# Five small moves in the two mixers of a two-layer decoder step

## The chip, the cores and the metric

The kernel runs on one core of a Trainium2 chip. The metric is the device time of one execution in microseconds; the times below are medians over runs.

## The reference

One inference step of two layers, for 512 prompt rows and 64 sample rows (8 sequences of 8) that share all weights. Everything is float32.

Layer 0 has a mixer of two halves behind one input projection. Four retention heads: queries and keys are rotated, and o = intra + cross, a chunkwise linear attention with decay in chunks of 128 rows and a carried state; then o is normalised by `rsqrt(mean(o*o))` over its 128 channels and gated by silu(g). Four gMLP groups: a layer norm of gelu(gv), then within chunks of 128 rows `u * (tril(W_s) v + b)`. Both halves go through one output projection. Layer 1 is grouped attention with a window of 128, 16 query heads, 2 key/value heads and sinks. Each layer adds a residual, then an RMS norm and a squared-ReLU MLP with 4096 hidden channels, and another residual. A final RMS norm follows.

```python
h = x + mixer(rmsnorm(x))          # layer 0: mixer_ab, layer 1: swa
h = h + square(relu(rmsnorm(h) @ w_up)) @ w_down
o = o * rsqrt(mean(o*o) + eps); o_ret = silu(g) * o
o_gm = gelu(u) * (tril(w_s) @ layernorm(gelu(gv)) + b_s)
```

## The kernel before

All 576 rows lie along the free dimension, channels on the 128 partitions, in 8 chunks of 128 channels. To keep float32 precision, every operand of a large product is split into a high and a low part (`whi`, `wlo` for weights, `xhi`, `xlo` and so on for data), and a product is three matmuls: high x high, high x low, low x high. ScalarE casts the high part (L272 for weights), VectorE subtracts it from the source for the low part (L283). A weight piece is 128x512, two pieces make one chunk of output; six pieces can be held.

`gemm(xs)` makes one chunk of 128 output channels: 8 input chunks x 3 parts x 2 column halves of 288 = 48 matmuls. It writes an accumulator of two PSUM banks; there are two accumulators (tag acc), and four single banks (tag m) for everything else. `gemm` can be given other output banks by its argument `outs`, and functions to call between its input chunks by `mid`.

`chunk(xs, evac)` is one gemm, the evacuation of its accumulator, and then `stages()`, which calls what was put off with `later(d, fn)` until this many chunks on. So the small work of a head or a group is traced behind the large products of later chunks.

The program text is not the order in which an engine works. Outside the MLPs and one short stretch, where VectorE and ScalarE keep the order of the text, a planner sets the order of each engine's instructions, DMA issues included, when the kernel is built: it goes by its own model of durations and takes what its operands, buffers and banks allow, the earlier in the text first. On the chip each engine then runs its list in that fixed order and waits wherever an operand is late.

First mixer (`mixer0`): the chunks come as values 0, keys 0, values 1, queries 0, keys 1, queries 1, then values, keys and queries of heads 2 and 3, then `gv_out` of the four groups, `gate_out` of the four heads, `u_out` of the four groups, then the output projection. For a head, `scores` is traced one chunk after its queries, `mix` one chunk after that, and `normalise` one chunk after `mix`. `mix` leaves the head's output oT and its square osq (L886); `normalise` calls `mean_rsqrt`, which first splits osq into `sqh` (L220, ScalarE) and `sql` (L221, VectorE), multiplies both by a matrix of ones (L398, L399, TensorE) and takes the inverse root. Scaling oT by it is GpSimd's work, as are the sums of the rotations (L745), the decayed queries (L815) and the masked values vm (L783, for the samples' states). Work tiles of 576 columns share one tag with 21 slots.

For a group, `layernorm` is traced one chunk after `gv_out`: transposes to two single banks (L751), statistics, the normalised group gvn (L928, VectorE, out of the two banks), and GpSimd's scale and shift (L934, L936). gvn has three buffers. `spatial`, three chunks later, multiplies each group by the masked matrix wst (L945) and ws8, and VectorE adds the bias into om (L949, L952). The masks are two GpSimd products in place (L980, L982), traced right after the loads of wst and ws8, behind queries 0.

Second mixer (`mixer1`): the keys' chunk, then the values' chunk, both into accumulators, then query chunks 0 to 7. Within the values' gemm, at its fifth input chunk, `keys` is called: it finishes the norm, scales the keys (L1034), adds the bias and splits them. `v_out` scales the values (`scaled`, L1024), adds the bias (L1049), and puts off their transposes (L1054), which are traced within query chunk 0. Each query chunk belongs to one head of either key/value group. `scores` of a query chunk is traced two chunks on, `transpose_p` three chunks on, each in four parts, one for each half of the rows and key/value group; ScalarE copies the transposed probabilities of the first half out of PSUM (L1156), VectorE those of the second (L1158). `softmax` works in between (L1090 to L1105: maxima on VectorE, exponentials on ScalarE, the scaling on GpSimd). `values` is traced four chunks on.

Of the kernel before, what the change touches and what calls it, by code (L numbers as in the profile page):

```python
# [14 lines left out]
ALU = mybir.AluOpType  # L15
# [3 lines left out]
P = 128  # L19
# [3 lines left out]
NS = 64  # L23
# [96 lines left out]
def hybrid_step(ctx: ExitStack, tc: tile.TileContext, a, o):  # L120
# [6 lines left out]
    def halves(ap):  # L127
        return ap.rearrange("p (a b) -> p a b", a=2)

    def half(hf):  # L130
        return slice(hf * TH, (hf + 1) * TH)
# [232 lines left out]
    def later(d, fn):  # L364
        due.setdefault(slot[0] + d, []).append(fn)
# [10 lines left out]
    def chunk(xs, evac):  # L376
        evac(gemm(xs))
        stages()
# [8 lines left out]
    def two_parts(sq, temp):  # L387
        hi, lo = temp("sqh", F32R), temp("sql", F32R)
        split_into(sq, hi, lo)
        return hi, lo  # L390

    def mean_rsqrt(ones_r, sq, out, temp, parts_=None):

        hi, lo = parts_ or two_parts(sq, temp)
        r0, x = temp("rs0"), temp("rsx")
        for hf in range(2):
            ms = m_tile("ms")
            nc.tensor.matmul(ms[:, 0:TH], lhsT=ones_r, rhs=hi[:, half(hf)], start=True, stop=False)  # L398
            nc.tensor.matmul(ms[:, 0:TH], lhsT=ones_r, rhs=lo[:, half(hf)], start=False, stop=True)  # L399
            nc.scalar.activation(out=r0[:, half(hf)], in_=ms[:, 0:TH], func=AF.Abs_reciprocal_sqrt, bias=eps_r)  # L400
            nc.vector.scalar_tensor_tensor(out=x[:, half(hf)], in0=ms[:, 0:TH], scalar=RMS_EPS, in1=r0[:, half(hf)],
                                           op0=ALU.add, op1=ALU.mult)
        newton(x, r0, out)
# [273 lines left out]
    def mixer0(norm, nxt):  # L677
        with tc.tile_pool(name="mx0", bufs=2) as mp:
# [3 lines left out]
            def con(name):  # L682
                off, wd = C0W[name]
                return cst[:, off:off + wd]
# [173 lines left out]
            def mix(hd, qd, sd, sds, st, cxs):  # L858
                s0 = s0s[hd]
                (vt, vs, vms), (kt, k2) = vts[hd], kts[hd]  # L860
                g8 = float(pow_g(hd, DL))
                oT = w("oT")
                op_ = m_tile("op")
                for n in range(NB):
                    s_ = slice(n * P, (n + 1) * P)
                    nc.tensor.matmul(op_[:, s_], lhsT=vt[:, n, :], rhs=sd[:, n, :], start=True, stop=(n == 0))
                    if n > 0:
                        nc.tensor.matmul(op_[:, s_], lhsT=st[:, n - 1, :], rhs=qd[:, s_], start=False, stop=True)
                os_ = m_tile("os")
                nc.tensor.matmul(os_[:, 0:NS], lhsT=vs, rhs=sds, start=True, stop=False)  # L870
                for grp in range(2):
                    nc.tensor.matmul(os_[:, 32 * grp:32 * (grp + 1)], lhsT=cxs[:, grp, :], rhs=con("sel"),
                                     start=False, stop=(grp == 1))
                nc.scalar.copy(out=oT[:, 0:NP], in_=op_)
                nc.scalar.copy(out=oT[:, NP:T], in_=os_[:, 0:NS])
                for hf in range(2):
                    bs = slice(hf * 4, (hf + 1) * 4)
                    kvs = m_tile("kvs")
                    for i in range(2):
                        nc.tensor.matmul(kvs, lhsT=k2, rhs=vms[i][:, bs, :], start=(i == 0), stop=(i == 1))  # L880
                    nc.vector.scalar_tensor_tensor(out=s0[:, bs, :].rearrange("p b v -> p (b v)"),
                                                   in0=s0[:, bs, :].rearrange("p b v -> p (b v)"),
                                                   scalar=g8, in1=kvs, op0=ALU.mult, op1=ALU.add)
                nc.sync.dma_start(out=o["ret_s"][:, hd].rearrange("b d v -> d b v"), in_=s0)
                osq = w("osq")
                nc.scalar.activation(out=osq, in_=oT, func=AF.Square)  # L886

                def normalise():
                    ro = w("ro")
                    mean_rsqrt(ones_v, osq, ro, w)  # L890
                    nc.gpsimd.tensor_tensor(out=oT, in0=oT, in1=ro, op=ALU.mult)
                    ons[hd] = oT

                later(1, normalise)
# [17 lines left out]
            def layernorm(g, gz):  # L912
                tp, tq = to_tokens(gz)
                blocks = [(P, tp[:, n * P:(n + 1) * P]) for n in range(NB)] + [(NS, tq[0:NS, 0:P])]
                mv = mp.tile([P, NB + 1, 2], F32, name="mv", tag="mv")
                nc.gpsimd.memset(mv, 1.0)
                for n, (rows_, src) in enumerate(blocks):
                    bst = mp.tile([P, 6], F32, name="bst", tag="bst", bufs=4)
                    nc.vector.bn_stats(out=bst[0:rows_], in_=src)
                    nc.vector.bn_aggr(out=mv[0:rows_, n, :], in_=bst[0:rows_])  # L920
                var = mv[:, :, 1]
                r0, x, rl = (mp.tile([P, NB + 1], F32, name=n_, tag=n_) for n_ in ("rl0", "rlx", "rl"))
                nc.scalar.activation(out=r0, in_=var, func=AF.Abs_reciprocal_sqrt, bias=eps_l)
                nc.vector.scalar_tensor_tensor(out=x, in0=var, scalar=LN_EPS, in1=r0, op0=ALU.add, op1=ALU.mult)
                newton(x, r0, rl)
                gvn = mp.tile([P, NB + 1, P], F32, name="gvn", tag="gvn", bufs=3)
                for n, (rows_, src) in enumerate(blocks):
                    nc.vector.tensor_scalar(out=gvn[0:rows_, n, :], in0=src, scalar1=mv[0:rows_, n, 0:1],  # L928
                                            scalar2=rl[0:rows_, n:n + 1], op0=ALU.subtract, op1=ALU.mult)
                gs = slice(g * P, (g + 1) * P)  # L930
                for rows_, ns_ in ((P, slice(0, NB)), (NS, slice(NB, NB + 1))):
                    k = ns_.stop - ns_.start
                    v_ = gvn[0:rows_, ns_, :]
                    nc.gpsimd.tensor_tensor(out=v_, in0=v_, in1=ln_g[0:rows_, None, gs].broadcast_to([rows_, k, P]),  # L934
                                            op=ALU.mult)
                    nc.gpsimd.tensor_tensor(out=v_, in0=v_, in1=ln_b[0:rows_, None, gs].broadcast_to([rows_, k, P]),  # L936
                                            op=ALU.add)
                nc.sync.dma_start(out=o["gm"][:, gs], in_=gvn[0:NS, NB, :])
                later(3, lambda: spatial(g, gvn))

            def spatial(g, gvn):
                gs = slice(g * P, (g + 1) * P)
# [13 lines left out]
            def u_out(g, view):  # L956
# [20 lines left out]
            nc.sync.dma_start(out=wst, in_=a["wst"])  # L977
            ws8 = mp.tile([NS, NH, NS], F32, name="ws8", bufs=1)
            nc.sync.dma_start(out=ws8, in_=a["ws8"])
            nc.gpsimd.tensor_tensor(out=wst, in0=wst, in1=con("tri")[:, None, :].broadcast_to([P, NH, P]),  # L980
                                    op=ALU.mult)
            nc.gpsimd.tensor_tensor(out=ws8, in0=ws8,  # L982
                                    in1=con("tris")[0:NS, None, :].broadcast_to([NS, NH, NS]), op=ALU.mult)
            chunk(xs, lambda v: k_out(1, v))
            chunk(xs, lambda v: q_out(1, v))
            for hd in (2, 3):
                chunk(xs, lambda v: v_out(hd, v))
                chunk(xs, lambda v: k_out(hd, v))
                chunk(xs, lambda v: q_out(hd, v))
            for g in range(4):  # L990
                chunk(xs, lambda v: gv_out(g, v))
            for hd in range(4):
# [9 lines left out]
    def mixer1(norm, nxt):  # L1002
        with tc.tile_pool(name="mx1", bufs=2) as mp:
# [17 lines left out]

            def scaled(view):
                z = w("z")
                nc.vector.tensor_tensor(out=halves(z), in0=view, in1=norm.rv, op=ALU.mult)  # L1024
                return z

            kview = gemm(xs)
# [39 lines left out]

                later(1, tokens)

            v_out(gemm(xs, mid={4: [keys]}))  # L1070
            stages()


# [72 lines left out]
            def transpose_p(c, kv, np_):  # L1146
                s = ss[c, kv][0]
                if np_ == 0:
                    pts[c, kv] = mp.tile([P, NB, 2, P], F32, name="pT", tag="pT", bufs=3)
                tp = m_tile("tpp")  # L1150
                for i in range(1 if np_ == 0 else 0, 4):
                    n, hf = 2 * np_ + i // 2, i % 2
                    nc.tensor.transpose(out=tp[:, i * P:(i + 1) * P], in_=s[:, n, hf * P:(hf + 1) * P], identity=ident)  # L1153
                dst = pts[c, kv][:, 2 * np_:2 * np_ + 2].rearrange("p n h i -> p (n h i)")
                if np_ == 0:
                    nc.scalar.copy(out=dst[:, P:512], in_=tp[:, P:512])  # L1156
                else:
                    nc.vector.tensor_copy(out=dst, in_=tp)  # L1158

# [247 lines left out]
```

## Time and profile before

| | |
|---|---|
| Median of three runs | 1215.81 us (1213.68 to 1215.82) |
| Profiled execution | 1217.04 us; its span, first to last instruction, 1215.2 us |
| TensorE busy | 1190.1 us, 98% of the span |
| VectorE, ScalarE, GpSimd busy | 869.1, 576.8, 156.1 us |
| Mean granted TensorE clock | 0.994 of full speed |
| DMA | 109.42 MB, 90 GB/s over the span |

The span runs from the first to the last instruction of the profiled execution. Idle time of an engine is put down to what released it. In the span, the first mixer lies at about 0 to 268 us, the first MLP at 268 to 642, the second mixer at 642 to 826, the second MLP at 826 to the end.

### The profile page before, as it was taken

The page shows a single profiled execution, that of the slowest core. Times are in us where ns is not written, and L with a number is a line of the kernel's source. Part 1 is how long each engine was busy: PE and PEld are TensorE (multiplying, and loading weights), DVE is VectorE, ACT ScalarE, POOL GpSimd, SP SyncE. Part 2 cuts the span into 40 slices and gives each one's busy share as a digit, 9 for nine tenths or more (in the row PEclk, how much of TensorE's full clock was granted, in tenths as well). Part 3 has the DMA queues.
Part 4 walks back from the last instruction along what each step waited for, and adds up shares of the span by engine and source line. Part 5 has one row for each costly group of instructions (what it writes and reads, how often), then busy time and mean ns, then how long its engine had stood idle before and what let it go on. Part 6 is the DMA issues. An engine that isn't in the chain of part 4 may idle for free.

```text
span 1215.2 us, 22586 instructions
## 1 busy us (share of the span) xinstructions
PE 1190.1 (98%) x9177; PEld 1172.4 (96%) x9177; DVE 869.1 (72%) x1608; ACT 576.8 (47%) x1084; POOL 156.1 (13%) x137
## 2 busy tenths in 40 slices
PE   8999999999999999999999999999999999999996
PEld 8998999999999999999999989999999999999996
DVE  8967685447865875785796768646794795695696
ACT  6333554344443544453465777535453553453452
POOL 3443250110000000000001654120000000000000
PEclk9999999999999999999999999999999999999998
DMA  7244222222232232232223212122223132232222
GB/s 271 104 140 120 78 71 74 85 70 87 88 105 71 84 118 72 73 108 85 86 86 111 70 38 70 36 87 70 83 92 105 52 122 86 72 105 87 76 81 79
DMA packets 38263, 109.42 MB, mean 90 GB/s; under 512 B 4160, under 2 KB 12544, under 8 KB 38144
## 3 DMA queue, kind: packets, MB, share of 16 engines
q1 hardware_dynamic: 37440, 107.36, 28.7%
q8 instruction: 72, 1.18, 0.4%
q10 hardware_dynamic: 720, 0.62, 0.2%
q14 instruction: 31, 0.25, 0.1%
HBM read 102.92 MB, written 6.03 MB: 90 GB/s over the span
## 4 chain that ended last, share of the span: by engine, by line
PE 80%; DVE 11%; DMA 3%; ACT 3%; issue 2%; SPq 0%; DVEq 0%; ACTq 0%
PE acc L328 53%; PE acc L340 8%; PE f L340 3%; PE y L340 3%; PE w L340 3%; PE z L340 3%; DVE wlo L283 3%; DMA raw<-in_w_dn 2%; PE op L1166 1%; PE tpp L1153 1%; DVE alo L499 1%; PE sp L1134 1%; ACT ahi L498 1%; DVE h L547 1%; PE dn L328 1%
## 5 line engine op out<-in xcount | busy, mean ns | idle before, releaser
L328 PE MATMUL acc<-xhi,whi 128*128 128x288 f32 x1520 | 326.0, 296 | 2.6 <-DVE z L1034 2.2
L328 PE MATMUL acc<-xhi,wlo 128*128 128x288 f32 x1520 | 323.6, 294 | 0.0
L328 PE MATMUL acc<-xlo,whi 128*128 128x288 f32 x1520 | 322.5, 294 | 0.0
L283 DVE TENSOR_TENSOR wlo<-raw,whi 128x512 fp32r<-128x512 f32 x321 | 227.7, 722 | 80.9 <-ACT whi L272 79.4
L272 ACT CAST whi<-raw 128x512 fp32r<-128x512 f32 x321 | 191.4, 617 | 143.5 <-PE acc L328 109.5
L328 PEld LDWEIGHTS acc<-xhi,whi 128*128 128x128 f32 x1520 | 242.8, 189 | 4.3 <-issue 3.8
L328 PEld LDWEIGHTS acc<-xhi,wlo 128*128 128x128 f32 x1520 | 243.7, 188 | 0.3
L328 PEld LDWEIGHTS acc<-xlo,whi 128*128 128x128 f32 x1520 | 243.2, 188 | 0.0
L495 ACT ACTIVATE q<-t 128x576 f32<-128x576 f32 x64 | 43.9, 685 | 229.6 <-DVE t L490 229.6
L490 DVE SCALAR_TENSOR_TENSOR t<-acc,rstd 128x576 f32<-128x576 f32 x64 | 48.3, 755 | 82.9 <-PE acc L328 82.7
L272 ACT CAST whi<-s 128x512 fp32r<-128x512 f32 x124 | 73.7, 619 | 65.3 <-DVE s L257 55.8
L283 DVE TENSOR_TENSOR wlo<-s,whi 128x512 fp32r<-128x512 f32 x124 | 83.4, 683 | 10.6 <-ACT whi L272 10.6
L499 DVE TENSOR_TENSOR alo<-q,ahi 128x864 fp32r<-128x864 f32 x64 | 77.1, 1205 | 8.3 <-ACT ahi L498 8.3
L498 ACT CAST ahi<-q 128x864 fp32r<-128x864 f32 x64 | 66.5, 1038 | 13.6 <-DVE q L506 12.6
L340 PE MATMUL acc<-ahi,wlo 128*128 128x288 f32 x340 | 71.3, 298 | 0.6
L340 PE MATMUL acc<-ahi,whi 128*128 128x288 f32 x340 | 71.4, 295 | 0.0
L340 PE MATMUL acc<-alo,whi 128*128 128x288 f32 x340 | 70.3, 295 | 0.0
L257 DVE TENSOR_TENSOR s<-raw 128x512 f32<-128x512 f32 x62 | 42.5, 686 | 19.7 <-DMA raw<-in_w_dn 19.7
L1041 POOL TENSOR_TENSOR kl<-z,kh 64x512 fp32r<-64x512 f32 x4 | 5.5, 1365 | 394.4 <-ACT kh L1038 394.2
L340 PEld LDWEIGHTS acc<-ahi,wlo 128*128 128x128 f32 x340 | 53.6, 188 | 2.5 <-DVE wlo L283 2.5
L340 PEld LDWEIGHTS acc<-ahi,whi 128*128 128x128 f32 x340 | 54.0, 188 | 0.0
L340 PEld LDWEIGHTS acc<-alo,whi 128*128 128x128 f32 x340 | 53.7, 188 | 0.0
(329 smaller groups left out, 2090.5 us busy)
## 6 DMA issues: line engine op xcount, KB each, us to landing
raw<-in_w_up SPq DMA_DIRECT2D x64, 512.0 KB
raw<-in_w_dn SPq DMA_DIRECT2D x64, 512.0 KB
raw<-in_w_in SPq DMA_DIRECT2D x22, 512.0 KB
raw<-in_w_o SPq DMA_DIRECT2D x16, 512.0 KB
raw<-in_w_qkv SPq DMA_DIRECT2D x10, 512.0 KB
h<-in_xT SPq DMA_DIRECT2D x8, 288.0 KB
s<-in_s SPq DMA_DIRECT2D x4, 512.0 KB
out_ret_s<-s SPq DMA_DIRECT2D x4, 512.0 KB
```

The source lines that it names most:

```text
L257: nc.vector.tensor_tensor(out=sums[k, i], in0=x, in1=b[y], op=ALU.add)
L272: nc.scalar.copy(out=hi, in_=src)
L283: nc.vector.tensor_tensor(out=lo, in0=src, in1=hi.bitcast(F32), op=ALU.subtract)
L328: nc.tensor.matmul(out, lhsT=w_, rhs=x_[:, hf if isinstance(hf, slice) else half(hf)], start=(start and si == 0), stop=(stop and si == 2))
L340: nc.tensor.matmul(out, lhsT=w[wi][:, k * P:(k + 1) * P], rhs=x(k)[xi], start=(start and n == 0), stop=(stop and n == len(steps) - 1), ski ...
L490: nc.vector.scalar_tensor_tensor(out=halves(t), in0=view, scalar=0.0, in1=norm.rv, op0=ALU.max, op1=ALU.mult)
L495: nc.scalar.activation(out=flat(q[:, seg]), in_=t, func=AF.Square)
L498: nc.scalar.copy(out=hi[:, s0 - 1:s1 - 1], in_=q[:, s0:s1])
L499: nc.vector.tensor_tensor(out=lo[:, s0 - 1:s1 - 1], in0=q[:, s0:s1], in1=hi.bitcast(F32)[:, s0 - 1:s1 - 1], op=ALU.subtract)
L547: nc.vector.tensor_tensor(out=row[:, cols_], in0=row[:, cols_], in1=src, op=op)
L1134: nc.tensor.matmul(sp[:, i * 256 + 256 - wd:(i + 1) * 256], lhsT=q[kv][:, n * P:(n + 1) * P], rhs=kst[kv][part][:, lo:lo + wd], start=(par ...
L1153: nc.tensor.transpose(out=tp[:, i * P:(i + 1) * P], in_=s[:, n, hf * P:(hf + 1) * P], identity=ident)
```

## The change

Five places, none of which changes what is computed.

1. In `mixer0`, `mix` splits osq into its two parts at once, and hands them to `normalise`, which ran the split itself, a chunk later in the text.
2. `spatial` is put off four chunks instead of three.
3. The two mask products stand after the queries of head 3 instead of after the loads.
4. In `mixer1` the values' gemm writes two single banks (`vview`) instead of an accumulator; `scaled` then takes two instructions, one for each half.
5. In `transpose_p` the copy of the first half of the rows goes to VectorE for query chunk 0, once for each key/value group, and stays on ScalarE for the others.

```diff
@@ mix
                 nc.scalar.activation(out=osq, in_=oT, func=AF.Square)
+                osq_parts = two_parts(osq, w)
 
                 def normalise():
                     ro = w("ro")
-                    mean_rsqrt(ones_v, osq, ro, w)
+                    mean_rsqrt(ones_v, osq, ro, w, osq_parts)
@@ layernorm
-                later(3, lambda: spatial(g, gvn))
+                later(4, lambda: spatial(g, gvn))
@@ mixer0
-            nc.gpsimd.tensor_tensor(out=wst, in0=wst, in1=con("tri")[:, None, :].broadcast_to([P, NH, P]),
-                                    op=ALU.mult)
-            nc.gpsimd.tensor_tensor(out=ws8, in0=ws8,
-                                    in1=con("tris")[0:NS, None, :].broadcast_to([NS, NH, NS]), op=ALU.mult)
             chunk(xs, lambda v: k_out(1, v))
             chunk(xs, lambda v: q_out(1, v))
             for hd in (2, 3):
                 chunk(xs, lambda v: v_out(hd, v))
                 chunk(xs, lambda v: k_out(hd, v))
                 chunk(xs, lambda v: q_out(hd, v))
+            nc.gpsimd.tensor_tensor(out=wst, in0=wst, in1=con("tri")[:, None, :].broadcast_to([P, NH, P]),
+                                    op=ALU.mult)
+            nc.gpsimd.tensor_tensor(out=ws8, in0=ws8,
+                                    in1=con("tris")[0:NS, None, :].broadcast_to([NS, NH, NS]), op=ALU.mult)
@@ scaled
-                nc.vector.tensor_tensor(out=halves(z), in0=view, in1=norm.rv, op=ALU.mult)
+                if isinstance(view, list):
+                    for hf in range(2):
+                        nc.vector.tensor_tensor(out=z[:, half(hf)], in0=view[hf], in1=norm.rv[:, hf], op=ALU.mult)
+                else:
+                    nc.vector.tensor_tensor(out=halves(z), in0=view, in1=norm.rv, op=ALU.mult)
@@ mixer1
-            v_out(gemm(xs, mid={4: [keys]}))
+
+            vview = [m_tile("v1")[:, 0:TH] for _ in range(2)]
+            gemm(xs, vview, mid={4: [keys]})
+            v_out(vview)
@@ transpose_p
-                if np_ == 0:
+                if np_ == 0 and c:
                     nc.scalar.copy(out=dst[:, P:512], in_=tp[:, P:512])
+                elif np_ == 0:
+                    nc.vector.tensor_copy(out=dst[:, P:512], in_=tp[:, P:512])
                 else:
                     nc.vector.tensor_copy(out=dst, in_=tp)
```

## Rows read from the trace of the kernel before

**Rows 1.** The page's busy times, in us, with shares and counts.

```profile
PE 1190.1 (98%) x9177; PEld 1172.4 (96%) x9177; DVE 869.1 (72%) x1608; ACT 576.8 (47%) x1084; POOL 156.1 (13%) x137
```

**Rows 2.** TensorE's timeline: start, us, operation, count, [idle before it <- releaser].

```profile
47.08 1.13 PE L831 MATMUL kv<-vt,kt 128*128 128x128 f32 x8 [1.30 <-DVE v2l L779]
...
92.22 0.53 PE L399 MATMUL ms<-sql,ones_v 128*128 128x288 f32 x2 [1.14 <-DVE sql L221]
...
120.67 0.54 PE L399 MATMUL ms<-sql,ones_v 128*128 128x288 f32 x2 [1.13 <-DVE sql L221]
...
161.77 0.63 PE L751 MATMUL tp<-ident,gvz 128*128 128x128 f32 x4 [0.23 <-DVE gvn L928]
...
166.80 1.13 PE L945 MATMUL mx<-wst,gvn 128*128 128x128 f32 x8 [0.58 <-DVE om L952]
...
657.50 0.50 PE L328 MATMUL acc<-xhi,whi 128*128 128x288 f32 x2 [2.23 <-DVE z L1034]
...
703.57 1.12 PE L1153 MATMUL tpp<-ident,s 128*128 128x128 f32 x4 [2.43 <-ACT pT L1156]
```

**Rows 3.** Windows: stretch, its length, busy us by engine, granted clock, DMA.

```profile
658.00:664.00 6.00, 6.00 (x36) 6.00 (x36) 1.45 (x2) 3.93 (x7) 4.93 (x4) 0.72 0.33 90
703.00:708.00 5.00, 4.43 (x24) 4.44 (x25) 3.90 (x11) 2.52 (x7) 1.85 (x3) 0.66 0.00 0
46.00:48.00 2.00, 0.92 (x8) 0.95 (x8) 1.96 (x5) 0.00 (x0) 0.00 (x0) 1.00 0.00 0
268.00:650.00 382.00, 381.48 (x2894) 379.62 (x2893) 288.20 (x497) 180.62 (x305) 0.00 (x0) 1.00 0.29 88
```

**Rows 4.** Timeline at the head of the second mixer.

```profile
656.59 0.76 DVE L1034 TENSOR_TENSOR z<-acc,rstd 128x576 f32<-128x576 f32 x1
...
657.87 0.75 DVE L1024 TENSOR_TENSOR z<-acc,rstd 128x576 f32<-128x576 f32 x1
...
662.43 0.78 ACT L1049 ACTIVATE z<-z,cols 128x576 f32<-128x576 f32 x1
...
663.71 0.60 PE L1054 MATMUL tp<-ident,z 128*128 128x128 f32 x4
```

**Rows 5.** Timeline of ScalarE, VectorE and GpSimd ahead of the 2.43 us gap.

```profile
690.31 0.83 ACT L1156 COPY pT<-tpp 128x384 f32<-128x384 f32 x2
...
691.14 1.83 POOL L1105 TENSOR_TENSOR s<-s,den 128x128 f32<-128x128 f32 x2 [0.37 <-ACT pT L1156]
...
691.70 1.81 DVE L283 TENSOR_TENSOR wlo<-raw,whi 128x512 fp32r<-128x512 f32 x1 [0.71 <-ACT whi L272]
...
693.43 0.68 DVE L1158 COPY pT<-tpp 128x512 f32<-128x512 f32 x1
...
697.94 0.40 ACT L1093 ACTIVATE s<-s,nmax 128x128 f32<-128x128 f32 x1 [0.88 <-DVE nmax L1090]
```

**Rows 6.** Timeline from the square of head 1 to its low part.

```profile
78.99 0.69 ACT L886 ACTIVATE osq<-oT 128x576 f32<-128x576 f32 x1
...
80.09 1.90 POOL L783 TENSOR_TENSOR vm<-v2h,cst 128x1024 fp32r<-128x1024 f32 x1 [0.65 <-DVE wlo L283]
...
83.25 1.15 DVE L283 TENSOR_TENSOR wlo<-raw,whi 128x512 fp32r<-128x512 f32 x1 [2.06 <-ACT whi L272]
...
87.79 0.66 ACT L220 CAST sqh<-osq 128x576 fp32r<-128x576 f32 x1
...
90.33 1.83 DVE L221 TENSOR_TENSOR sql<-osq,sqh 128x576 fp32r<-128x576 f32 x1
```

**Rows 7.** Timeline of GpSimd and VectorE around the masks.

```profile
13.14 0.15 POOL L916 MEMSET mv<- 128x10 f32 x2
...
36.19 1.74 POOL L980 TENSOR_TENSOR wst<-wst,cst 128x512 f32<-128x512 f32 x1
...
39.53 5.58 DVE L803 TENSOR_TENSOR k<-ks__513,k 64x128 fp32r<-64x128 f32 x1
...
57.88 0.27 DVE L803 TENSOR_TENSOR k<-ks__726,k 64x128 fp32r<-64x128 f32 x1
```

## Prediction, made before the changed kernel was run

> **What bounds the kernel now.** I read four views, from coarse to fine. First the page's busy line [rows 1]: TensorE is busy 1190.1 of the span's 1215.2 us, so all that can be won without taking matmuls away is 25 us, less what the start and the end need. Second the TensorE timeline, of which only the rows with idle time ahead of them matter [rows 2]. The seven inside the two mixers are what the five edits can reach: 1.30, 1.14, 1.13, 0.23 and 0.58 us in the first mixer, 2.23 and 2.43 us in the second, 9.04 us in all. Each names who ended it, always VectorE or ScalarE letting go of a PSUM bank or delivering an operand; no weight load and no DMA is among them. Third, windows around these gaps [rows 3]. After the 2.23 us gap the granted clock averages 0.72 over 6 us, so 6 x 0.28 = 1.7 us more is lost; after the 2.43 us gap it averages 0.66 over 5 us, 1.7 us, of which up to 0.57 is idle time already counted, so I take 1.4. The stretch with the 1.30 us gap stays at 1.00. So the two long gaps cost 3.9 and 3.8 us, the five short ones only themselves: 12.1 us in all. For scale, the first MLP, with no gap of note, runs 2894 matmuls in 382 us, 0.132 us each, so a chunk of 48 takes 6.3 us. Fourth, the other engines around each gap [rows 4 to 7].
>
> The reader must keep in mind that a planner sets each engine's order from readiness in its own model. The first two memsets of the layer norms ran at 13.14 us [rows 7], ahead of the first head's work. So an edit of the text moves an instruction only if its operands or its slot held it back.
>
> **Part by part, in the size of the prize.**
>
> *Values in single banks.* The third product of the second mixer (query chunk 0) needs one of two accumulators, and both are held: the keys' until z at L1034 (656.59 + 0.76 us), the values' until z at L1024 [rows 4]. TensorE idles 2.23 us [rows 2]. With the values in two of the four single banks, query chunk 0 takes the accumulator that the MLP has let go, and starts at once. No matmul is added. VectorE does the values' scaling in two instructions instead of one of 0.75 us; even at twice that it adds 0.75 us, hidden while TensorE works through 6.3 us of query chunk 0, and the bank it holds longer is asked for only by the transposes that read its own result. Gain 2.23 + 1.7 = 3.9 us. Lower bound 0: the next thing late is the values' activation L1049 (ready at 662.43 + 0.78 = 663.2), on which the transposes L1054 wait [rows 4]; that is a rival below.
>
> *One copy on VectorE.* The 2.43 us gap ends when the copies at L1156 free a bank [rows 2]; they stand behind a row of exponentials on ScalarE that begins at 697.94 [rows 5]. These are copies of query chunk 1; the edit moves those of chunk 0, two instructions that take 0.83 us of ScalarE at 690.31. What they delay is seen in the same rows: the weight split on VectorE begins at 691.70 and takes 1.81 us beside a GpSimd product, then a copy, which ends at 694.1, then the scaling of query chunk 3, its maxima, and the exponentials. If ScalarE is free 0.83 us sooner, this chain comes 0.83 us sooner; if the split then also gets ahead of the GpSimd product, 1.81 goes to about the 0.68 that its neighbour takes [rows 5], another 1.1 us. VectorE pays two copies of 384 columns. The 512-column copy took 0.68, so an estimate from this row is 0.5 us each, 1.0 in all; the planner can set them before the chunk's end, and if that cover is gone they eat the 0.83. A gap of 0.5 to 1.6 us remains, near the 1.30 one that cost no clock. So the gain lies between 0.83 + 1.4 = 2.2 and 1.9 + 1.4 = 3.3; I take 2.2. Bounds 0 and 3.8.
>
> *Heads' squares split sooner.* In head 1 the square ends at 78.99 + 0.69 = 79.7 us, but its high part is made only at 87.79, and the low part begins at 90.33 and takes 1.83 us [rows 6]. The mean's second matmul waits 1.14 us for it; head 2 repeats this with 1.13 [rows 2]. ScalarE was not full in those 8 us, so something other than its operands held the high part, and its place in the program, one chunk on, is the likely one: slots of the shared work pool seem to be given out in program order. Traced right behind the square, both parts are ready several microseconds ahead of the matmul. Nothing is added; two work tiles live a chunk longer. Gain 2.27. Lower bound: the low part now falls beside GpSimd's masked values (80.09) [rows 6], the second rival.
>
> *Spatial products a chunk later.* They free TensorE from waiting for the sums before them (0.58), and the transposes from waiting for banks held by them (0.23) [rows 2]: gain 0.81. But only three buffers hold the normalised groups, so group 3's norm must now wait for group 0's product. TensorE comes to that product where group 1's stood, 166.80 to 167.9 [rows 2]. VectorE ended group 2's norm at about 161.7, which is what released the transposes at 161.77 [rows 2], and group 3's comes a chunk of at least 6.3 us later, 168 or after. So the wait is hidden behind the work that VectorE has before that norm, and costs nothing; if VectorE is early, it is at most a chunk of 6.3 us on VectorE.
>
> *Masks later.* On GpSimd the mask of wst took 1.74 us at 36.19, in a row of GpSimd work during which VectorE's 64-partition subtraction at L803 took 5.58 us; the same line otherwise took 0.27 [rows 7]. That subtraction pushes the one that ends the 1.30 us gap [rows 2]. Without the mask the row would be shorter and the gap smaller. But the masks need only their load, the planner put them where GpSimd had nothing else ready, and a later place in the program changes neither. So I take 0; bound 1.30.
>
> **Sum.** 3.9 + 2.2 + 2.3 + 0.8 + 0 = 9.2 us. The profiled execution took 1217.04 us (1.84 beyond its span); the median of the three runs is 1215.81. From the median: 1206.6 us. The same case with all its upper bounds wins the whole 12.1: 1203.7; with the copy's gain at 0 and the squares' at half, 5.9, it gives 1210.0. A change of 0.2% is 2.4 us, about what a measurement of this kernel can tell from none.
>
> **Rivals.**
>
> *The gap moves to the transposes.* In favour: the vector and scalar work behind the keys does not get faster, and the values' activation is ready at 663.2, while TensorE, 3.9 us sooner, would reach the transposes (now at 663.71) at 659.8 [rows 4], so it would wait up to 3.4 us, and the dip of the clock would follow as it does now. Against: the planner sees the same lateness in its model and can put the rest of query chunk 0 ahead of the transposes. The first edit then gives nothing: 1215.8 - 5.3 = 1210.5 us.
>
> *Slower: the low parts meet GpSimd.* VectorE's low part, issued beside the masked values at 80.09, would be held as L803 was, 5.58 less its own 0.27, or 5.3 us; VectorE's idle time there is 2.06 [rows 6], so 3.2 us would reach the rotations and weight splits behind it, in each of four heads: 12.8 us, against 6.9 won elsewhere: 1215.8 + 5.9 = 1221.7 us. It decides from 1.7 us a head. Against: TensorE has 6.3 us of matmuls a chunk and split weights in hand, so a late VectorE must be later than that. The low part of head 1 in the trace took 1.83 us and not 5.58 [rows 6].
>
> The Trainium skill (SBUF — State Buffer, Who interferes with whom) bears on this rival: a VectorE instruction with two SBUF inputs and a GpSimd instruction that reads SBUF exclude each other, and the one issued second waits until the first has finished. By that rule a low part would be held for one masked product of 1.90 us, less than the idle 2.06 us, and the rival would give the forecast's time. The trace disagrees in L803's row: 5.58 us, about three times the longest GpSimd instruction in these rows. The price above goes by the row.
>
> *No change.* The planner puts squares, copies and spatial products where they were, or orders the rest so that other waits open; 1214 to 1218 us. In favour: order is not the text's. Against: the accumulator is a resource, not an order, and it alone is worth more than 2.4 us.
>
> **Chances.** The forecast 0.60 (its own range 1203.7 to 1210.5), the moved gap 0.19 (1209 to 1213), no change 0.12, slower 0.09. Faster by over 0.2%: 0.79; within: 0.12; slower: 0.09. A range of 1203.5 to 1214.5 leaves out the slower case, half of no change and a little of the forecast.
>
> **What would show it.** No gap at the start of query chunk 0 and a granted clock of 1.00 around it; the high part of each square directly behind the square, and no wait at the mean's second matmul; no wait at the spatial products; the masks still at 36 us and the 1.30 us gap still there; the 2.43 us gap under 1.6 without a dip of the clock. It is wrong if a gap of over 2 us shows at the values' transposes, if low parts of over 3 us show beside GpSimd with TensorE idle behind, or if new gaps add up to more than 3 us.

## The result: 1208.3 us after 1215.1, and the profile after

| | before | after |
|---|---|---|
| Median, run side by side | 1215.07 us (1213.68 to 1215.82, 4 runs) | 1208.33 us (1207.19 to 1210.16, 4 runs) |
| Profiled execution, its span | 1217.04, 1215.2 us | 1207.19, 1205.4 us |
| Mean granted TensorE clock in it | 0.994 | 0.998 |

The ratio is 0.993, 95% interval 0.9915 to 0.9946: faster by 0.5% to 0.9%. The forecast was 1206.6 us in 1203.5 to 1214.5, so the range holds and the middle is 1.7 us too low. All runs of the study pooled, before has a median of 1216.31 us (40 runs, lowest 1213.68) and after one of 1208.33 (10 runs, lowest 1206.82). The medians of the table are 6.7 us apart, the pooled ones 8.0, and the interval of the ratio reaches from 6.6 to 10.3 us: the times alone give the gain to about 2 us.

The page's busy line answers to [rows 1]:

```profile
PE 1186.1 (98%) x9177; PEld 1169.3 (97%) x9177; DVE 872.6 (72%) x1611; ACT 576.4 (48%) x1082; POOL 157.6 (13%) x137
```

The same 9177 matmuls take 4.0 us less busy time: matmuls at half clock count as longer. Of TensorE's timeline, what is left of the seven gaps of [rows 2]:

```profile
47.05 1.13 PE L831 MATMUL kv<-vt,kt 128*128 128x128 f32 x8 [1.30 <-DVE v2l L779]
...
86.64 0.30 PE L399 MATMUL ms<-sql,ones_v 128*128 128x288 f32 x1
...
650.69 0.43 PE L328 MATMUL v<-xhi,wlo 128*128 128x288 f32 x2
650.96 0.42 PE L328 MATMUL acc<-xhi,whi 128*128 128x288 f32 x2
...
658.05 0.66 PE L1059 MATMUL tp<-ident,z 128*128 128x128 f32 x4 [1.07 <-ACT z L1054]
...
695.38 0.66 PE L1161 MATMUL tpp<-ident,s 128*128 128x128 f32 x4 [1.07 <-ACT pT L1164]
```

The mean's second matmul follows the first without a wait. Query chunk 0 (into acc, 650.96) follows the values (into v) directly. Gone are 1.14, 1.13, 0.23, 0.58 and 2.23 us; 2.43 has become 1.07; a new wait of 1.07 stands at the values' transposes; 1.30 is untouched. The seven gaps of 9.04 us are now three of 3.44. The window with the new wait, which answers to the first of [rows 3], shows no loss of clock:

```profile
655.00:661.00 6.00, 4.93 (x39) 4.69 (x39) 2.07 (x4) 4.71 (x10) 5.37 (x4) 1.00 0.31 98
```

So the profiled span is 9.8 us shorter: 5.6 in gaps, 3.1 in clock that is no longer lost, and 1.1 outside these waits. Most of this 1.1 is in the first mixer: TensorE comes to the mean of the first MLP's norm (L398) at 263.24 us instead of 267.21, 3.97 sooner, and the waits that are gone there are 1.14 + 1.13 + 0.23 + 0.58 = 3.08 of it. What the rest consists of I did not locate.

ScalarE's timeline around the new wait, and GpSimd's, VectorE's and ScalarE's around the squares and the copies, which answer to [rows 4 to 6]:

```profile
654.15 2.53 ACT L1043 CAST kh<-z 64x512 fp32r<-64x512 f32 x4
656.71 0.62 ACT L272 CAST whi<-raw 128x512 fp32r<-128x512 f32 x1
657.23 0.77 ACT L1054 ACTIVATE z<-z,cols 128x576 f32<-128x576 f32 x1
...
79.02 0.69 ACT L886 ACTIVATE osq<-oT 128x576 f32<-128x576 f32 x1
79.80 0.68 ACT L220 CAST sqh<-osq 128x576 fp32r<-128x576 f32 x1
...
80.19 1.90 POOL L783 TENSOR_TENSOR vm<-v2h,cst 128x1024 fp32r<-128x1024 f32 x1 [0.64 <-DVE wlo L283]
...
81.21 1.49 DVE L221 TENSOR_TENSOR sql<-osq,sqh 128x576 fp32r<-128x576 f32 x1
...
684.09 0.55 DVE L1166 COPY pT<-tpp 128x384 f32<-128x384 f32 x1
...
684.64 0.66 DVE L283 TENSOR_TENSOR wlo<-raw,whi 128x512 fp32r<-128x512 f32 x1
...
694.85 0.85 ACT L1164 COPY pT<-tpp 128x384 f32<-128x384 f32 x2
```

The values' bias is in ScalarE's queue behind four key casts and a weight cast. The high part of the square stands right behind the square, and the weight split after the moved copy takes 0.66 us, not 1.81. And GpSimd and VectorE, which answer to [rows 7]:

```profile
36.16 1.74 POOL L987 TENSOR_TENSOR wst<-wst,cst 128x512 f32<-128x512 f32 x1
...
39.49 5.58 DVE L803 TENSOR_TENSOR k<-ks__513,k 64x128 fp32r<-64x128 f32 x1
...
46.33 0.57 DVE L779 TENSOR_TENSOR v2l<-tq,v2h 64x128 fp32r<-64x128 f32 x2
```

The masks are where they were, and VectorE's subtraction at L803 takes 5.58 us as before.

### The profile page after: what moved, and what is told of

It is laid out like the page before. It is cut to its first block, busy times and chain, and to the rows that moved or that the text cites. A ratio compares the mean times of both kernels' runs of the same rounds, so it can differ in the third digit from the quotient of the medians.

```text
span 1205.4 us, 22593 instructions
## 1 busy us (share of the span) xinstructions
PE 1186.1 (98%) x9177; PEld 1169.3 (97%) x9177; DVE 872.6 (72%) x1611; ACT 576.4 (48%) x1082; POOL 157.6 (13%) x137
## 4 chain that ended last, share of the span: by engine, by line
PE 82%; DVE 10%; ACT 3%; DMA 3%; issue 2%; SPq 0%; DVEq 0%; ACTq 0%
PE acc L328 54%; PE acc L340 8%; PE f L340 3%; PE y L340 3%; PE w L340 3%; PE z L340 3%; DVE wlo L283 2%; DMA raw<-in_w_dn 2%; ACT s L1101 1%; PE tpp L1161 1%; DVE alo L499 1%; PE op L1176 1%; DVE h L547 1%; PE sp L1142 1%; ACT ahi L498 1%
## 5 line engine op out<-in xcount | busy, mean ns | idle before, releaser
L328 PE MATMUL acc<-xhi,whi 128*128 128x288 f32 x1504 | 321.4, 295 | 0.4 <-DVE vz L765 0.4
L328 PE MATMUL acc<-xhi,wlo 128*128 128x288 f32 x1504 | 319.0, 293 | 0.0
L328 PE MATMUL acc<-xlo,whi 128*128 128x288 f32 x1504 | 318.7, 293 | 0.0
L283 DVE TENSOR_TENSOR wlo<-raw,whi 128x512 fp32r<-128x512 f32 x321 | 232.2, 736 | 76.2 <-ACT whi L272 74.7
L328 PEld LDWEIGHTS acc<-xhi,whi 128*128 128x128 f32 x1504 | 239.3, 188 | 1.6 <-issue 1.2
L328 PEld LDWEIGHTS acc<-xhi,wlo 128*128 128x128 f32 x1504 | 240.4, 188 | 0.3
L328 PEld LDWEIGHTS acc<-xlo,whi 128*128 128x128 f32 x1504 | 240.0, 188 | 0.0
L499 DVE TENSOR_TENSOR alo<-q,ahi 128x864 fp32r<-128x864 f32 x64 | 77.1, 1205 | 8.3 <-ACT ahi L498 8.3
```

The lines of the kernel that those rows point to most:

```text
L283: nc.vector.tensor_tensor(out=lo, in0=src, in1=hi.bitcast(F32), op=ALU.subtract)
L328: nc.tensor.matmul(out, lhsT=w_, rhs=x_[:, hf if isinstance(hf, slice) else half(hf)], start=(start and si == 0), stop=(stop and si == 2))
L499: nc.vector.tensor_tensor(out=lo[:, s0 - 1:s1 - 1], in0=q[:, s0:s1], in1=hi.bitcast(F32)[:, s0 - 1:s1 - 1], op=ALU.subtract)
```

## The experiments

**One part undone at a time.** Four kernels, each the changed one with one of its parts taken back; run side by side, with before at a median of 1216.75 us.

Values back in an accumulator:

```diff
-            vview = [m_tile("v1")[:, 0:TH] for _ in range(2)]
-            gemm(xs, vview, mid={4: [keys]})
-            v_out(vview)
+            v_out(gemm(xs, mid={4: [keys]}))
```

> The changed kernel with the values' product back in an accumulator. Theory that each edit is worth its own gap: the 2.23 us gap at the start of query chunk 0 is back, with the dip of the clock behind it (1.7 us), and the 1.07 us gap at the values' transposes goes: 1208.3 + 2.2 - 1.1 + 1.7 = 1211.2 us. Rival, that the gap only moved from the accumulator to the transposes: at most 0.5 us either way, 1208.3 us.

Measured: 1210.46 us (1209.81 to 1211.8; ratio to before 0.9951, 0.9933 to 0.9968). TensorE's timeline, then two windows:

```profile
653.37 0.51 PE L328 MATMUL acc<-xhi,whi 128*128 128x288 f32 x2 [2.13 <-DVE z L1039]
```

```profile
653.00:659.00 6.00, 5.63 (x31) 5.66 (x32) 1.75 (x4) 4.16 (x7) 4.06 (x4) 0.72 0.32 90
760.00:768.00 8.00, 8.00 (x92) 6.93 (x89) 2.09 (x6) 1.64 (x7) 1.82 (x2) 0.79 0.01 2
```

The gap returns in place of the wait at the transposes, with a dip of 0.28 x 6 = 1.7 us behind it. The second row shows a dip of the same size (0.21 x 8) at 760 us, where before's profile and after's have none, and no gap of over 0.3 us ahead of it.

Squares split where they were, inside `mean_rsqrt`:

```diff
-                osq_parts = two_parts(osq, w)
-                    mean_rsqrt(ones_v, osq, ro, w, osq_parts)
+                    mean_rsqrt(ones_v, osq, ro, w)
```

> The changed kernel with the heads' squares split in normalise again. Theory of own gaps: 1.14 and 1.13 us come back at the mean's second matmul in heads 1 and 2, no dip: 1208.3 + 2.3 = 1210.6 us. Rival, that the early low parts cost VectorE beside GpSimd what they save TensorE: 1208.3 us or less.

Measured: 1210.25 us (1208.99 to 1213.15; ratio 0.9949, 0.9931 to 0.9968). TensorE's timeline, and a window:

```profile
92.23 0.53 PE L399 MATMUL ms<-sql,ones_v 128*128 128x288 f32 x2 [1.14 <-DVE sql L221]
...
120.69 0.54 PE L399 MATMUL ms<-sql,ones_v 128*128 128x288 f32 x2 [1.13 <-DVE sql L221]
```

```profile
762.00:768.00 6.00, 6.00 (x59) 5.28 (x61) 1.87 (x6) 1.61 (x6) 0.50 (x1) 0.72 0.00 0
```

Both waits are back to the hundredth, and a dip at 762 us stands in this profile too.

Spatial products three chunks on:

```diff
-                later(4, lambda: spatial(g, gvn))
+                later(3, lambda: spatial(g, gvn))
```

> The changed kernel with the spatial products three chunks on again. Theory of own gaps: 0.58 and 0.23 us come back in front of the second spatial product and of group 3's transposes: 1208.3 + 0.8 = 1209.1 us. Rival, that the wait of group 3's norm for a buffer costs more than that: 1208.3 us or less.

Measured: 1210.39 us (1210.12 to 1211.89; ratio 0.995, 0.9932 to 0.9969), more than expected. TensorE's timeline:

```profile
159.63 0.63 PE L751 MATMUL tp<-ident,gvz 128*128 128x128 f32 x4 [0.80 <-DVE gvn L929]
...
164.66 1.13 PE L946 MATMUL mx<-wst,gvn 128*128 128x128 f32 x8 [0.58 <-DVE om L953]
```

1.38 us of waits return, of which 0.80 is at the transposes where before had 0.23: without the squares' wait ahead of it, TensorE comes to the transposes sooner (the kernel before with only the squares' waits gone, below, has the same 0.80). A gap behind another one is larger once the first is gone.

The copies of query chunk 0 back on ScalarE:

```diff
-                if np_ == 0 and c:
+                if np_ == 0:
                     nc.scalar.copy(out=dst[:, P:512], in_=tp[:, P:512])
```

> The changed kernel with query chunk 0's copies on ScalarE again. Theory of own gaps: the gap at the transposes of query chunk 1 grows from 1.07 to 2.43 us and brings back its dip of 1.4 us: 1208.3 + 2.8 = 1211.1 us. Rival, that this gap shrank because the second mixer starts earlier by the values' edit: no change, 1208.3 us.

Measured: 1209.07 us (1207.84 to 1211.97; ratio 0.9941, 0.9922 to 0.996). TensorE's timeline and a window:

```profile
697.54 0.66 PE L1161 MATMUL tpp<-ident,s 128*128 128x128 f32 x4 [2.43 <-ACT pT L1164]
```

```profile
697.00:703.00 6.00, 5.46 (x44) 5.46 (x45) 5.93 (x17) 3.70 (x9) 3.17 (x4) 1.00 0.16 25
```

The gap is back at its old size, with the values' edit still in, so it was the copies and not the earlier start that had shrunk it. The clock stays at 1.00. The price of this edit is here the gap alone, 1.36 us, of which the medians show 0.7; with a spread of 4 us between runs that is no disagreement, and no proof either.

What the four give beside 1208.33 us is 2.1, 1.9, 2.1 and 0.7 us. But the changed kernel did not run in this comparison, and the four intervals overlap, so the times alone do not price the parts. The clock takes out much of the spread: each execution has its span and its mean granted clock, and (1 - clock) x span is an estimate of what the clock cost it. With this taken off, the mean time is 1204.0 us for the changed kernel (10 executions) and 1204.9, 1206.5, 1206.4 and 1205.5 us with the values, the squares, the spatial products and the copies undone (6 each): 0.9, 2.6, 2.5 and 1.5 us more, the third to about 0.5 and the others to about 0.3. The waits in the traces gave 2.13 - 1.07 = 1.06, 2.27, 1.38 and 1.36; the figure for the spatial products lies 1.1 above their waits, twice its error, which settles nothing. The four together are 7.5 us, and the whole change, by the same estimate, 7.2: the parts add up.

The masks have no run of their own: with them put back behind the loads, the built program has the same instructions in the same order on every engine.

**The same kernel again, and why the order moved.** The next four ran side by side (before 1217.33 us median, 15 runs).

> The changed kernel once more, as the yardstick for the three beside it. Every theory expects its 1208.3 us again, with TensorE's two new waits of 1.07 us in the second mixer (the values' transposes, and the transposes of the probabilities). The theory that the loss of clock after a wait comes and goes between executions expects executions whose mean clock differs by some thousandths, the longer ones at the lower clock; if each wait had its fixed price, all executions would show one clock.

Measured: 1208.33 us (1206.82 to 1210.01; ratio 0.9924, 0.9908 to 0.994). Its six runs had mean clocks of 0.997, 0.997, 0.996, 0.996, 0.996 and 0.995 in the order of their times. Before's fifteen run from 1213.69 us at 0.997 to 1219.56 at 0.993. The loss of clock comes and goes. The three waits of this kernel are 1.32, 1.03 and 1.08 us in the second trace, 1.30, 1.07 and 1.07 in the first.

In the kernel before, with the place of the split left alone:

```diff
-NW = 21
+NW = 19
-                    mean_rsqrt(ones_v, osq, ro, w)
+                    mean_rsqrt(ones_v, osq, ro, w, two_parts(
+                        osq, lambda n_, dt: mp.tile([P, T], dt, name=n_, tag="sqp", bufs=2)))
```

> The kernel before with the call that splits the squares left where it stood, but with the two parts in two tiles of their own; the shared work pool gives up two of its 21 slots for them. Theory A, the split comes late because a tile of the shared pool is granted in the order of the text: the split moves to right behind the squares although its text has not moved, the waits of 1.14 and 1.13 us at the mean's second matmul go, and the time falls as by that edit alone, by 2.3 us to about 1212.8 to 1214. Theory B, the place in the text decides by itself: same order, same waits, 1215 to 1217. A third, that two slots fewer hurt: slower than before, with new waits for slots on the engines that write the shared pool.

Measured: 1213.87 us (1210.72 to 1216.18, 10 runs; ratio 0.997, 0.9955 to 0.9985). Theory A holds. ScalarE's and TensorE's timelines of its profile, and two windows:

```profile
79.19 0.69 ACT L886 ACTIVATE osq<-oT 128x576 f32<-128x576 f32 x1
79.91 0.68 ACT L220 CAST sqh<-osq 128x576 fp32r<-128x576 f32 x1
...
159.79 0.63 PE L751 MATMUL tp<-ident,gvz 128*128 128x128 f32 x4 [0.80 <-DVE gvn L929]
...
655.48 0.51 PE L328 MATMUL acc<-xhi,whi 128*128 128x288 f32 x2 [2.07 <-DVE z L1035]
...
700.27 0.66 PE L1154 MATMUL tpp<-ident,s 128*128 128x128 f32 x4 [2.43 <-ACT pT L1157]
```

```profile
655.00:661.00 6.00, 5.52 (x43) 5.55 (x44) 2.29 (x4) 4.72 (x8) 4.00 (x3) 1.00 0.30 90
700.00:706.00 6.00, 5.73 (x46) 5.74 (x47) 5.96 (x17) 3.71 (x8) 3.45 (x4) 1.00 0.20 51
```

The cast stands behind the square with the text unmoved, so it was the shared pool's slot that held it. The waits of 1.14 and 1.13 us are gone, and the one at the transposes has grown from 0.23 to 0.80. This kernel still has gaps of 2.07 and 2.43 us in the second mixer, and neither is followed by a dip in this execution, of 1210.72 us. Its slowest took 1216.18 at a mean clock of 0.993. So gaps like the two that cost 3.1 us of clock in the profile that I worked from (the second is as long, the first 0.16 us shorter) can also cost none.

**What the new waits are made of.** The values' bias on VectorE:

```diff
-                nc.scalar.activation(out=vT, in_=vT, func=AF.Identity, bias=bq[:, 9:10])
+                nc.vector.tensor_scalar(out=vT, in0=vT, scalar1=bq[:, 9:10], scalar2=None, op0=ALU.add)
```

> The changed kernel with the bias of the second mixer's values added on VectorE in place of ScalarE. Theory A, the new 1.07 us wait at the values' transposes is ScalarE's queue (four key casts of 2.53 us in sum and a weight cast stand ahead of the 0.77 us bias): VectorE stands idle there for 2.7 us, the bias is done by about 655.5, the wait goes, and the time falls by about 1.1 us to 1207.2. Theory B, the transposes then wait for something else (the transposed keys, or the copies of the values behind them): the wait shrinks to about half or moves on by under a microsecond, and the time stays within 0.5 us of the changed kernel's.

Measured: 1210.19 us (1208.7 to 1212.72; ratio 0.994, 0.9923 to 0.9956): 1.9 us slower than the changed kernel beside it, which neither theory had said, though the two intervals overlap. Timelines of ScalarE, VectorE and TensorE, and two windows:

```profile
654.66 2.53 ACT L1043 CAST kh<-z 64x512 fp32r<-64x512 f32 x4
657.21 1.34 ACT L272 CAST whi<-raw 128x512 fp32r<-128x512 f32 x2
...
657.86 0.69 DVE L283 TENSOR_TENSOR wlo<-raw,whi 128x512 fp32r<-128x512 f32 x1 [2.71 <-ACT whi L272]
658.47 1.52 DVE L1054 TENSOR_SCALAR z<-z,cols 128x576 f32<-128x576 f32 x1
...
660.09 0.63 PE L1059 MATMUL tp<-ident,z 128*128 128x128 f32 x4 [2.19 <-issue]
...
660.00:666.00 6.00, 5.91 (x46) 5.94 (x47) 2.25 (x4) 3.68 (x7) 3.21 (x3) 1.00 0.10 28
761.00:767.00 6.00, 6.00 (x61) 5.42 (x61) 2.10 (x6) 1.64 (x7) 0.00 (x1) 0.72 0.01 3
```

VectorE idles 2.71 us, but in order: ahead of the bias stands a weight split that waits for a weight cast, which waits on ScalarE behind the same four key casts. The bias has changed engines and kept its queue. The wait at the transposes has grown by 1.2 us, from 1.03 in the changed kernel's trace beside it; no loss of clock follows it in this execution, and a dip of 1.7 us stands at 761 us instead.

So the casts themselves were moved, in the changed kernel:

```diff
+            def key_parts():
                 for kv, kr in enumerate(rows_of):
                     for ds_ in rows_of:
                         nc.scalar.copy(out=kst[kv][0][ds_], in_=kT[kr, 0:NP])
...
             v_out(vview)
+            key_parts()
             stages()
```

The rest of the loop, the low parts, moves with them.

> The changed kernel with the four key casts on ScalarE (2.53 us in sum) put behind the bias of the second mixer's values; nothing is left out. Theory A, these casts in ScalarE's queue are what the new 1.07 us wait at the values' transposes consists of, also where the bias itself stood on VectorE (there its queue's weight part waited for a weight cast behind the same four): the wait goes, and the time falls by about 1 us to 1207.3, provided that the low parts of the keys on GpSimd still come before the first scores. Theory B, the casts are only pushed in front of the copies of the values and of the first query chunk: the wait appears at the first scores instead, about 1 us, and the time stays within 0.5 us of 1208.3.

Measured: 1207.24 us (1206.06 to 1209.47; ratio 0.9928, 0.9911 to 0.9945; before beside it 1215.92). ScalarE's timeline, and TensorE's:

```profile
654.40 0.62 ACT L1045 CAST kh<-z 64x512 fp32r<-64x512 f32 x1
654.92 0.78 ACT L1056 ACTIVATE z<-z,cols 128x576 f32<-128x576 f32 x1
655.72 1.88 ACT L1045 CAST kh<-z 64x512 fp32r<-64x512 f32 x3
...
655.75 0.65 PE L1061 MATMUL tp<-ident,z 128*128 128x128 f32 x4
```

One cast ahead of the bias instead of four, and the wait at the transposes is gone, with none at the first scores: theory A. The time is 1.1 us under the changed kernel's, run in another comparison (before 1215.92 us here, 1217.33 there).

Copies of query chunk 1 on VectorE too:

```diff
-                if np_ == 0 and c:
+                if np_ == 0 and c > 1:
                     nc.scalar.copy(out=dst[:, P:512], in_=tp[:, P:512])
```

> The changed kernel with the copies of the first pair's probabilities on VectorE for query chunk 1 as well as for chunk 0. Theory A, what is left of the old 2.43 us gap (1.07 us, the transposes of the probabilities wait for ScalarE's copy of chunk 1, which starts only when ScalarE has done its exponentials and the cast of the output's high part): VectorE is idle at 693.1 to 694.6, takes the copy there, the wait shrinks to under 0.3 us and the time falls by about 0.8 to 1.1 us to 1207.3. Theory B, VectorE's own queue holds the copy (its sums of the exponentials wait for ScalarE until 694.6, and the low part of the output, 0.69 us, stands behind them): the wait stays near 1 us with VectorE as its releaser and the time does not move.

Measured: 1206.73 us (1205.84 to 1208.39; ratio 0.9912, 0.9895 to 0.9929), 1.6 us under the changed kernel beside it. VectorE's timeline and TensorE's:

```profile
692.64 0.55 DVE L1166 COPY pT<-tpp 128x384 f32<-128x384 f32 x1
...
695.40 0.30 PE L1142 MATMUL sp<-kh,q 128*128 128x128 f32 x1 [0.28 <-DVE olo L221]
...
706.40 0.66 PE L1161 MATMUL tpp<-ident,s 128*128 128x128 f32 x4 [0.43 <-ACT pT L1164]
```

The copy goes where VectorE idled, and 1.08 us becomes 0.28 there, plus 0.43 a chunk later: theory A by the trace. These waits account for 0.4 of the 1.6 us; the intervals of the two ratios overlap, and the rest is not explained.

Masks in tiles of the shared pool, in the changed kernel:

```diff
+            wsm = w("wsm")[:, 0:512].rearrange("p (g c) -> p g c", g=NH)
-            nc.gpsimd.tensor_tensor(out=wst, in0=wst, ...
+            nc.gpsimd.tensor_tensor(out=wsm, in0=wst, ...
```

and the same for ws8; `spatial` reads the new tiles.

> The changed kernel with the two masked matrices written into tiles of the shared work pool in place of being written over the loaded ones. Theory A, the change's move of the masks did nothing because their operands come from a load and no tile had to be granted, so that they run as soon as GpSimd is free, and a tile of the shared pool ties them to their place in the text: the masks leave 36.2 us and come behind the third pair of heads; GpSimd's unbroken run there ends 2.4 us sooner, the k row that VectorE needs 5.58 us for (L803) ends sooner by about that much, the wait of 1.30 us at the kv products shrinks to under 0.4, and the time falls by about 1 us from 1208.3 to 1207.3. Theory B, GpSimd's other work holds VectorE just as long without the masks: L803 stays over 5 us, the wait stays, and the time does not move. A third: the masks, now late, meet the spatial products and TensorE waits there.

Measured: 1207.47 us (1206.55 to 1209.43; ratio 0.9932, 0.9914 to 0.995), 0.9 us under the changed kernel, but in another comparison: by the times alone this would be open, the trace decides it. Timelines of GpSimd, VectorE and TensorE:

```profile
37.62 1.90 POOL L783 TENSOR_TENSOR vm<-v2h,cst 128x1024 fp32r<-128x1024 f32 x1 [1.37 <-ACT v2h L777]
...
39.54 1.50 DVE L803 TENSOR_TENSOR k<-ks__513,k 64x128 fp32r<-64x128 f32 x1
41.06 3.99 DVE L283 TENSOR_TENSOR wlo<-raw,whi 128x512 fp32r<-128x512 f32 x2
44.97 0.57 DVE L779 TENSOR_TENSOR v2l<-tq,v2h 64x128 fp32r<-64x128 f32 x2
...
45.69 1.13 PE L831 MATMUL kv<-vt,kt 128*128 128x128 f32 x8
```

The masks now keep their place in the text (that of wst runs at 118.2 us), and the wait of 1.30 us is gone. The way there was not the expected one: GpSimd's work ends at 45.2 us as before, since it first waits 1.37 us for the values' high part. But VectorE gets L803 done in 1.50 us, and the hold falls on the weight splits behind it, two in 3.99; the subtraction that ends the wait comes at 44.97 instead of 46.33.

All three together:

> Three edits on top of the changed kernel: the masks in tiles of the shared pool, the key casts behind the bias of the values, and the copies of query chunk 1 on VectorE as well (which alone brought 1206.7 beside 1208.3). If the three waits are separate, the gains add: 1.6 and about 1 and about 1, so 1204.5 to 1205.2. If one of the first two gives nothing, 1205.7; if both give nothing, 1206.7.

Measured: 1204.67 us (1203.83 to 1204.84, 4 runs; ratio to before 0.9903, 0.9885 to 0.9922), the fastest version here, 3.7 us under the changed kernel, which ran in other comparisons; the expectation for three gains that add was 1204.5 to 1205.2. The wait at the kv products is gone. What remains in the second mixer on TensorE:

```profile
653.85 0.66 PE L1063 MATMUL tp<-ident,z 128*128 128x128 f32 x4 [0.52 <-ACT z L1058]
...
693.47 0.30 PE L1147 MATMUL sp<-kh,q 128*128 128x128 f32 x1 [0.28 <-DVE olo L221]
...
704.47 0.66 PE L1166 MATMUL tpp<-ident,s 128*128 128x128 f32 x4 [0.40 <-ACT pT L1169]
```

## Why the prediction was right, and where its size was off

**Values in single banks.** The accumulators were what query chunk 0 waited for; undone, the gap is back with the same releaser. The rival of the moved gap came true in part. It put the wait at up to 3.4 us; it is 1.07, without a dip. The reason given against it holds: the planner set 44 of query chunk 0's 48 matmuls ahead of the transposes, 35 before. The term had nothing for this wait: it won 2.23 - 1.07 = 1.16 us in gaps, not 2.23.

**The copy.** 0.83 was the lower of the two values given. The weight split did get ahead of the GpSimd product (0.66 us for 1.81), so the gap shrank by 1.36.

**Squares.** 2.27 us predicted, both waits gone. The reason given, that slots of the shared pool go out in program order, is shown by the kernel in which the text of the split stays where it was and only the slots change.

**Spatial.** 0.81 us predicted and seen; undone alone it costs 1.38, the difference being the squares' wait that no longer covers the transposes. The three buffers of the normalised groups cost TensorE no wait.

**Masks.** Right that nothing moves: the work has no tile to be granted, so a later line holds back nothing. This is the one part in which the rival of no change came true.

**The slower rival.** Low parts beside GpSimd's masked values took 1.49 us, 2.45 at most, not 5.3. The Trainium skill (SBUF — State Buffer, Who interferes with whom) has the second wait until the first is done; here the masked values end at 80.19 + 1.90 = 82.09, and the low part at 81.21 + 1.49 = 82.70. The trace agrees with that rule in this place, and its price would have been the better one.

**The term that was mis-sized is the clock.** The sum took 1.7 + 1.4 = 3.1 us for the dips behind the two long gaps as if each execution paid them, and took that from a median. In the pair of profiles they did give 3.1, because before's profiled execution, 1217.04 us, had both; but a gap of 2.43 us can pass with the clock at 1.00, and a dip of the same 1.7 us can appear at 760 us with no long gap ahead. The estimate from each execution's clock, (1 - clock) x span, has a mean of 5.7 us in the 36 executions of before that have their clock on record, and of 4.5 us in the changed kernel's ten. (Both figures hold some 3 us of a stretch at the very end, 0.50 in 1209 to 1215 us before and in 1200 to 1205 us after without a matmul in it, so that only their difference counts.) So the clock gave about 1.2 us, to 0.5 or so, and not 3.1.

The other terms came out too low in sum: without the clock's loss the mean times fell from 1211.2 to 1204.0 us, by 7.2, where the terms had 2.23 + 0.83 + 2.27 + 0.81 = 6.1. The traces show 5.6 of it in gaps (the values' term 1.07 short, the copy's 0.53 over) and 1.1 outside them, for which the sum had nothing: 6.7, near 7.2. By these means the change is worth 7.2 + 1.2 = 8.4 us against a forecast of 9.2. That the middle came out so near is in part luck: 1.9 us too much for the clock stands against 1.1 too little elsewhere. What decides whether a dip follows a gap isn't settled; no run here separates it from chance.

## What to carry to other kernels

A stall's own length came back within 0.05 us when the same kernel ran again; what the clock loses differs from execution to execution. Price the two apart, and read the second from the clock of many executions, not from one profile. Before moving a line, ask what holds the instruction: an operand, a bank, or a slot that is granted in the order of the text; only the held ones move. And moving a late instruction to an idle engine helps only if nothing in that engine's order waits for the queue you left.

## What the hardware showed that was not expected

- Dips are of one size: the window of 6 us reads 0.72 after before's gap of 2.23 us [rows 3], after 2.13 with the values undone, at 762 us with the squares undone, and at 761 us with the bias on VectorE. Each is 1.7 us; the last two have no wait of over 0.3 us in the 50 us ahead of them.
- A gap of 2.43 us was followed by a dip in before, and by 1.00 in two other kernels; one of 2.19 us also by 1.00.
- VectorE's subtraction of two 64x128 tiles was held 5.58 us across several GpSimd instructions that ran without a break, in before and after alike; with a break of 1.37 us ahead of GpSimd's run, the same line took 1.50, and each weight split behind it about 2. What decides between one long hold and several short ones stays open.
